# Small attention matmuls of a hybrid decoder step on one core: head pairs, key pages and column groups issued side by side

## The chip, the core and the metric

The kernel runs on one core of a Trainium2 chip. A core has a matrix engine (TensorE, PE in the profile; its weight loads are listed apart, as PEld), VectorE (DVE), ScalarE (ACT), GpSimd (POOL), a queue engine that starts transfers (SP), and 16 DMA engines. Operands lie in SBUF, matmul results in PSUM, which has eight banks of 128 partitions by 512 fp32 columns. The metric is the device time of one execution, in microseconds; lower is better. Before the change it is 897.04 us (median of three runs, 896.72 to 897.54).

## The reference

One decoder layer for 512 prompt tokens and for 8 sequences that each add 4 tokens to 1024 cached ones. Three causal branches work on the same input and are merged by gates; a SwiGLU feed-forward follows. What matters here is the pooling branch's projection and the stick-breaking attention:

```
br_a = einsum('btgc,gcd->btgd', p, pool_w) * pool_scale        # 4 groups, 64 channels each
z    = einsum('bqhd,bkhd->bhqk', q, k) * HEAD_DIM**-0.5 + sb_bias
log_rest = where(mask, log_sigmoid(-z), 0)                     # mask: k_pos < q_pos
log_pass = cumsum(log_rest, axis=3, reverse=True) - log_rest
a    = where(mask, exp(log_sigmoid(z) + log_pass), 0)
o    = einsum('bhqk,bkhd->bqhd', a, v)                         # 8 heads of 64
merged = gate0 * br_a + gate1 * (o @ w_att_o) + gate2 * br_c
```

For the prompt the keys are the prompt's own, in blocks of 128 queries. For the 8 sequences they are 8 pages of 128 keys from a paged cache and the 4 new ones.

## The kernel before

**Large matmuls.** Nearly all of TensorE's work goes through one helper, `gemm` (the matmul of L223). An fp32 product is made of three passes in a rounded fp32 type: weight high part by data high part, high by low, low by high. Weights are streamed: a raw tile is loaded from HBM, ACT makes its high part (L131), DVE its low part (L132), and the two wait in one of three buffers. Data is held for all 544 tokens (32 sample tokens, then 512 of the prompt) and used in two halves of 288 and 256 columns. In the profile these are the rows `mm<-xh,wh`, `mm<-xl,wh`, `mm<-xh,wl`.

**Order.** The code is recorded in program order, and a scheduler then sets the order of each engine's instructions once, at build time, by its own picture of when each is ready. On the chip every engine takes its list from the front; an instruction that waits holds up what is behind it on that engine. Large matmuls that are ready are placed between the small ones of the attention.

**PSUM.** While the branches run, the eight banks are three for `mm`, two for `z`, two for `tp` and one for `o`.

**Projection of the pooling branch** (L492 to L501). Four groups contract over 64 channels only. For each of 8 output chunks and both halves of the tokens three matmuls (L499) of 64 rows go into a `z` bank, and ACT scales the result into `mg` (L501). Groups 0 and 2 lie in rows 0 to 63, groups 1 and 3 in rows 64 to 127. DVE meanwhile makes the depthwise convolution, one tap at a time (L426, `acc`).

**Prompt attention** (L553 to L608). A unit is a pair of heads and a block of 128 queries; 16 units. `front` makes the scores of the two heads `s`, three matmuls each over 64 rows (L564), head 0 in rows 0 to 63 and head 1 in rows 64 to 127, each into a `z` bank; DVE adds bias and mask (L565), then come logs, a reversed running sum (L572) and an exponential. `back`, one unit later, transposes the weights of each head (L583), ACT copies them (L584), and per head and key block a matmul (L586) makes 64 output rows of the one `o` bank. fp32 matmuls show as two rows each in the profile.

**Sample attention** (L619 to L729). For each sequence `k_load` fetches the keys in four tiles `kr`, each with two indirect transfers of 128 x 512 fp32 (256 KB) issued by POOL (L623); there are six such buffers, so one sequence and a half. `v_load` fetches the values in two tiles `vr` of 1 MB (L630), two buffers. `sample_front` makes the scores: for each of four head pairs `hp` and four tiles `jj` a matmul (L654) with 32 output rows, `jj` choosing which 32 (a column group of the array). `sample_back` makes the output from eight key blocks in the same four column groups (L680), and the new tokens' values as one matmul of 32 rows by 512 columns into the fourth group (L681). L668 and L687 are small matmuls of the running sum and of the head selection. Gate matmuls (L223) of the other branches run in between.

Of the kernel before, what the change touches and what calls it, by code (L numbers as in the profile page):

```python
# [146 lines left out]
def hybrid_layer_kernel(  # L147
# [14 lines left out]
           "z": psA.enter_context(pool("z", 2, space=PSUM)),  # L162
# [5 lines left out]
    def bank(tag="mm"):  # L168
        return pst[tag].tile([P, 512], F32, tag=tag, name=tag)

    def auxb():
        return bank("tp")

# [52 lines left out]
    # constants  # L226
# [266 lines left out]
    for mo in range(KD):  # L493
        g, m = mo // 2, mo % 2
        rs = 64 * (g % 2)
        for c0, c1 in HALVES:
            ps = bank("z")
            for n_, (a, b) in enumerate(((pw[0], ph_), (pw[0], pl_), (pw[1], ph_))):
                nc.tensor.matmul(ps[:, :c1 - c0], a[rs:rs + 64, g // 2, m * P:(m + 1) * P], b[rs:rs + 64, g // 2, c0:c1],  # L499
                                 start=n_ == 0, stop=n_ == 2)  # L500
            nc.scalar.mul(mg[:, mo, c0:c1], ps[:, :c1 - c0], vcol(V_PS + mo))  # L501
# [51 lines left out]
    def front(ap, hp, i, q_, k_):  # L553
# [4 lines left out]
        rc = ap.tile([P, 2, wd], F32, tag=f"rc{i % 2}", bufs=1, name=f"rc{hp}{i}", padded_shape=[P, 2, P * (3 + i % 2)])  # L558
        for s in range(2):
            r = slice(64 * s, 64 * s + 64)  # L560
            zp = bank("z")
            qs = slice(i * P, (i + 1) * P)
            for n_, (a, b) in enumerate(((qh, kh), (qh, kl), (ql, kh))):
                nc.tensor.matmul(zp[:, :wd], a[r, qs], b[r, :wd], start=n_ == 0, stop=n_ == 2)  # L564
            nc.vector.scalar_tensor_tensor(out=zt[:, s], in0=zp[:, :wd], scalar=vcol(V_SB + 2 * hp + s),  # L565
                                           in1=cc_(C_ME + NP - wd, wd), op0=ALU.add, op1=ALU.add)
# [10 lines left out]
    def back(ap, hp, i, rc, vtok):  # L577
        op_ = bank("o")
        for s in range(2):
            tp = bank("tp").rearrange("p (k c) -> p k c", k=4)  # L580
            at = ap.tile([P, 4, P], F32, tag="at", bufs=3, name=f"at{hp}{i}{s}")
            for kb in range(i + 1):
                nc.tensor.transpose(tp[:, kb], rc[:, s, kb * P:(kb + 1) * P], ident)  # L583
            nc.scalar.copy(at[:, :i + 1], tp[:, :i + 1])  # L584
            for kb in range(i + 1):
                nc.tensor.matmul(op_[64 * s:64 * s + 64, :P], vtok[:, kb, 64 * s:64 * s + 64], at[:, kb], start=kb == 0, stop=kb == i)  # L586
# [49 lines left out]
    def new_keys():  # L636
        znf = sp.tile([32, 256], F32, name="znf")
        znt = sp.tile([32, 256], F32, name="znt")
        zp = bank("z")
# [10 lines left out]
    def sample_front(b):  # L650
        zp = bank("z")
        for hp in range(4):
            for jj in range(4):
# [22 lines left out]
    def sample_back(b, at):  # L676
        op_ = bank("o")
        for j in range(8):
            c = j % 4
            nc.tensor.matmul(op_[32 * c:32 * c + 32], at[:, j], kvt[b, "v", j // 4][:, j % 4], start=j < 4, stop=j >= 4 and c < 3)  # L680
        nc.tensor.matmul(op_[96:128], at[96:128, 8], vs96[96:128], start=False, stop=True)  # L681
# [394 lines left out]
```

## Time and profile before

| | |
|---|---|
| median of three runs | 897.04 us |
| profiled execution, first to last instruction | 899.0 us |
| PE busy | 877.0 us (98%) |
| DVE, ACT, POOL busy | 478.1, 348.5, 134.8 us |
| share of the chain that ended last on PE | 96% |

The page's own span, 899.0 us, is 2.0 us above the median of the runs; sums below are made against the span and then set against the median. PE counts as busy from a matmul's start to its modelled end, and matmuls overlap, so a busy PE is not one that could take no more: what a matmul costs its successors is read from the distance between starts. The stages, from the timeline: input projections to about 47 us; the pooling projection between large matmuls, 47 to 78 us; prompt attention, 90 to 235 us; sample attention, 240 to 400 us; attention output, output projection and norm, to 501 us; feed-forward, to the end.

### The profile page before, as it was taken

The page shows a single profiled execution, that of the slowest core. Times are in us where ns is not written, and L with a number is a line of the kernel's source. Part 1 is how long each engine was busy: PE and PEld are TensorE (multiplying, and loading weights), DVE is VectorE, ACT ScalarE, POOL GpSimd, SP SyncE. Part 2 cuts the span into 40 slices and gives each one's busy share as a digit, 9 for nine tenths or more (in the row PEclk, how much of TensorE's full clock was granted, in tenths as well). Part 3 has the DMA queues.
Part 4 walks back from the last instruction along what each step waited for, and adds up shares of the span by engine and source line. Part 5 has one row for each costly group of instructions (what it writes and reads, how often), then busy time and mean ns, then how long its engine had stood idle before and what let it go on. Part 6 is the DMA issues. An engine that isn't in the chain of part 4 may idle for free.

```text
span 899.0 us, 16259 instructions
## 1 busy us (share of the span) xinstructions
PE 877.0 (98%) x6889; PEld 811.0 (90%) x6889; DVE 478.1 (53%) x845; ACT 348.5 (39%) x583; POOL 134.8 (15%) x158
## 2 busy tenths in 40 slices
PE   7999999999999999999999999999999999999993
PEld 6999999887886667779999999999999999999993
DVE  4899886887343454449646433333333333334437
ACT  5445377776533315244513333232323232222211
POOL 1430100005257476310001000000000000000002
PEclk9999999999999999999999999999999999999997
DMA  9314323214648688646610122233232322323322
GB/s 291 118 34 115 96 73 113 65 38 137 214 143 289 238 290 291 229 136 225 207 48 1 48 68 76 92 95 94 94 95 94 95 58 73 101 75 83 96 81 100
DMA packets 96393, 110.36 MB, mean 123 GB/s; under 512 B 4416, under 2 KB 88224, under 8 KB 94144
## 3 DMA queue, kind: packets, MB, share of 16 engines
q1 hardware_dynamic: 87840, 73.12, 26.4%
q0 software_dynamic: 8480, 36.20, 11.9%
q8 instruction: 54, 0.88, 0.4%
q14 instruction: 19, 0.16, 0.1%
HBM read 104.44 MB, written 4.87 MB: 122 GB/s over the span
## 4 chain that ended last, share of the span: by engine, by line
PE 96%; DVE 2%; ACT 1%; DMA 1%; issue 0%; SPq 0%; another core or an unknown queue 0%; DVEq 0%; ACTq 0%
PE mm L223 82%; PE z L654 3%; PE o L680 2%; PE z L564 2%; PE o L586 2%; PE tp L583 1%; PE tp L795 1%; PE o L681 1%; PE z L499 1%; DMA raw<-in_w_in 1%; PE tp L861 1%; DVE y L999 0%; DVE y L991 0%; PE tp L687 0%; DVE rc L572 0%
## 5 line engine op out<-in xcount | busy, mean ns | idle before, releaser
L132 DVE TENSOR_TENSOR wl<-raw,wh 128x1024 fp32r<-128x1024 f32 (+1 forms) x129 | 152.3, 1184 | 137.7 <-ACT wh L131 136.5
L131 ACT CAST wh<-raw 128x1024 fp32r<-128x1024 f32 (+1 forms) x129 | 129.3, 1006 | 238.9 <-PE mm L223 212.2
L223 PE MATMUL mm<-xh,wh 128*128 128x256 f32 (+1 forms) x672 | 198.3, 295 | 5.7 <-ACT wh L131 5.6
L223 PE MATMUL mm<-x1l,wh 128*128 128x288 f32 (+1 forms) x704 | 202.7, 288 | 0.0
L223 PE MATMUL mm<-x1h,wl 128*128 128x288 f32 (+1 forms) x704 | 201.4, 287 | 0.0
L223 PE MATMUL mm<-x1h,wh 128*128 128x288 f32 (+1 forms) x704 | 200.5, 286 | 0.1
L223 PE MATMUL mm<-xl,wh 128*128 128x256 f32 (+1 forms) x672 | 198.1, 295 | 0.2 <-DVE xl L210 0.2
L223 PE MATMUL mm<-xh,wl 128*128 128x288 f32 (+1 forms) x672 | 197.0, 294 | 0.7 <-issue 0.7
L223 PEld LDWEIGHTS mm<-xh,wh 128*128 128x128 f32 x672 | 127.9, 191 | 16.9 <-issue 9.8
L223 PEld LDWEIGHTS mm<-xl,wh 128*128 128x128 f32 x672 | 127.8, 190 | 8.6 <-issue 7.3
L223 PEld LDWEIGHTS mm<-xh,wl 128*128 128x128 f32 x672 | 127.5, 190 | 8.6 <-issue 7.7
L223 PEld LDWEIGHTS mm<-x1l,wh 128*128 128x128 f32 x704 | 132.2, 188 | 0.2
L223 PEld LDWEIGHTS mm<-x1h,wh 128*128 128x128 f32 x704 | 132.0, 188 | 0.4 <-ACT sg L905 0.3
L223 PEld LDWEIGHTS mm<-x1h,wl 128*128 128x128 f32 x704 | 132.0, 188 | 0.0
L223 PE MATMUL mm<-gl,wh 128*128 128x256 f32 (+1 forms) x352 | 101.7, 289 | 0.0
L223 PE MATMUL mm<-gh,wh 128*128 128x256 f32 (+1 forms) x352 | 101.3, 288 | 0.0
L223 PE MATMUL mm<-gh,wl 128*128 128x256 f32 (+1 forms) x352 | 100.8, 286 | 0.0
L623 POOL DMA_INDIRECT kr<-in_ck,pix x64 | 67.6, 1056 | 44.7 <-PE z L654 20.6
L908 DVE TENSOR_TENSOR sg<-mm,sg 128x288 f32<-128x288 f32 (+1 forms) x44 | 19.4, 441 | 91.8 <-PE mm L223 91.8
L223 PEld LDWEIGHTS mm<-gl,wh 128*128 128x128 f32 x352 | 66.1, 188 | 0.1
L223 PEld LDWEIGHTS mm<-gh,wh 128*128 128x128 f32 x352 | 66.2, 188 | 0.0
L223 PEld LDWEIGHTS mm<-gh,wl 128*128 128x128 f32 x352 | 66.1, 188 | 0.0
(216 smaller groups left out, 1202.8 us busy)
## 6 DMA issues: line engine op xcount, KB each, us to landing
raw<-in_w_in SPq DMA_DIRECT2D x14, 1024.0 KB, 8.2
raw<-in_w_g SPq DMA_DIRECT2D x11, 1024.0 KB, 5.3
raw<-in_w_u SPq DMA_DIRECT2D x11, 1024.0 KB, 5.4
raw<-in_w_d SPq DMA_DIRECT2D x16, 512.0 KB, 4.0
raw<-in_w_in SPq DMA_DIRECT2D x12, 512.0 KB, 3.9
raw<-in_w_out SPq DMA_DIRECT2D x4, 1024.0 KB
raw<-in_w_d SPq DMA_DIRECT2D x8, 384.0 KB, 4.3
raw<-in_w_att_o SPq DMA_DIRECT2D x4, 512.0 KB, 3.4
```

Source lines behind the costliest of these rows:

```text
L131: self.nc.scalar.copy(hi[:, a:b], v[:, a:b])
L132: self.nc.vector.tensor_tensor(out=lo[:, a:b], in0=v[:, a:b], in1=hi[:, a:b].bitcast(F32), op=ALU.subtract)
L223: ins = nc.tensor.matmul(ps[:, :n], lw, rr, start=first and s == 0, stop=last and s == len(steps) - 1)
L499: nc.tensor.matmul(ps[:, :c1 - c0], a[rs:rs + 64, g // 2, m * P:(m + 1) * P], b[rs:rs + 64, g // 2, c0:c1], start=n_ == 0, stop=n_ == 2)
L564: nc.tensor.matmul(zp[:, :wd], a[r, qs], b[r, :wd], start=n_ == 0, stop=n_ == 2)
L583: nc.tensor.transpose(tp[:, kb], rc[:, s, kb * P:(kb + 1) * P], ident)
L586: nc.tensor.matmul(op_[64 * s:64 * s + 64, :P], vtok[:, kb, 64 * s:64 * s + 64], at[:, kb], start=kb == 0, stop=kb == i)
L623: nc.gpsimd.indirect_dma_start(out=kr[:, u].rearrange("p h c -> p (h c)"), out_offset=None, in_=ck, in_offset=bass.IndirectOffsetOnAxis(ap ...
L654: nc.tensor.matmul(zp[32 * jj:32 * jj + 32, :256], qbd[:, hp, b], kvt[b, "k", jj][:, :, hp], start=hp == 0, stop=hp == 3)
L680: nc.tensor.matmul(op_[32 * c:32 * c + 32], at[:, j], kvt[b, "v", j // 4][:, j % 4], start=j < 4, stop=j >= 4 and c < 3)
L681: nc.tensor.matmul(op_[96:128], at[96:128, 8], vs96[96:128], start=False, stop=True)
L908: nc.vector.tensor_tensor(out=sg, in0=pu[:, :n], in1=sg, op=ALU.mult)
```

## The change

Five edits. The pool `z` has one buffer, a tile of two banks (`pair`), in place of two of one bank; `new_keys` and `sample_front` use its first bank. The pooling projection takes the two groups of a pair of row halves together: for each of three passes first the one group, then the other, and the second group's result is scaled by DVE, not ACT. `front` issues pass by pass over both heads, not head by head. `back` makes both heads' transposes and copies first (four `at` buffers, not three) and then the output matmuls block by block over both heads, head 1 first. `sample_front` takes the tiles `jj` in the order 3, 2, 1, 0, `sample_back` the second value tile before the first, and the new tokens' values are four matmuls of 128 columns, one per column group. The deleted comment lines of the diff are left out here.

```diff
-           "z": psA.enter_context(pool("z", 2, space=PSUM)),
+           "z": psA.enter_context(pool("z", 1, space=PSUM)),
...
+    def pair():
+        return pst["z"].tile([P, 2, 512], F32, tag="z", name="z")
...
-    for mo in range(KD):
-        g, m = mo // 2, mo % 2
-        rs = 64 * (g % 2)
-        for c0, c1 in HALVES:
-            ps = bank("z")
-            for n_, (a, b) in enumerate(((pw[0], ph_), (pw[0], pl_), (pw[1], ph_))):
-                nc.tensor.matmul(ps[:, :c1 - c0], a[rs:rs + 64, g // 2, m * P:(m + 1) * P], b[rs:rs + 64, g // 2, c0:c1],
-                                 start=n_ == 0, stop=n_ == 2)
-            nc.scalar.mul(mg[:, mo, c0:c1], ps[:, :c1 - c0], vcol(V_PS + mo))
+    for gp in range(2):
+        for m in range(2):
+            for hf, (c0, c1) in enumerate(HALVES):
+                zz = pair()
+                pss = [zz[:, s] for s in range(2)]
+                for n_, (a, b) in enumerate(((pw[0], ph_), (pw[0], pl_), (pw[1], ph_))):
+                    for s in range(2):
+                        r = slice(64 * s, 64 * s + 64)
+                        nc.tensor.matmul(pss[s][:, :c1 - c0], a[r, gp, m * P:(m + 1) * P], b[r, gp, c0:c1], start=n_ == 0, stop=n_ == 2)
+                for s in range(2):
+                    mo = 4 * gp + 2 * s + m
+                    if s:
+                        nc.vector.tensor_scalar(mg[:, mo, c0:c1], pss[s][:, :c1 - c0], vcol(V_PS + mo), None, op0=ALU.mult)
+                    else:
+                        nc.scalar.mul(mg[:, mo, c0:c1], pss[s][:, :c1 - c0], vcol(V_PS + mo))
...
+        zz = pair()
+        zps = [zz[:, s] for s in range(2)]
+        qs = slice(i * P, (i + 1) * P)
+        for n_, (a, b) in enumerate(((qh, kh), (qh, kl), (ql, kh))):
+            for s in range(2):
+                r = slice(64 * s, 64 * s + 64)
+                nc.tensor.matmul(zps[s][:, :wd], a[r, qs], b[r, :wd], start=n_ == 0, stop=n_ == 2)
...
+        for kb in range(i + 1):
+            for s in (1, 0):
+                nc.tensor.matmul(op_[64 * s:64 * s + 64, :P], vtok[:, kb, 64 * s:64 * s + 64], ats[s][:, kb], start=kb == 0, stop=kb == i)
...
-            for jj in range(4):
+            for jj in (3, 2, 1, 0):
...
-        for j in range(8):
+        for j in (4, 5, 6, 7, 0, 1, 2, 3):
             c = j % 4
-            nc.tensor.matmul(op_[32 * c:32 * c + 32], at[:, j], kvt[b, "v", j // 4][:, j % 4], start=j < 4, stop=j >= 4 and c < 3)
-        nc.tensor.matmul(op_[96:128], at[96:128, 8], vs96[96:128], start=False, stop=True)
+            nc.tensor.matmul(op_[32 * c:32 * c + 32], at[:, j], kvt[b, "v", j // 4][:, j % 4], start=j >= 4, stop=False)
+        for c in range(4):
+            f = slice(P * c, P * c + P)
+            nc.tensor.matmul(op_[32 * c:32 * c + 32, f], at[96:128, 8], vs96[96:128, f], start=False, stop=True)
```

What the scheduler makes of it is shown at three places. In the changed kernel `gemm`'s matmul is L226, and the others are named as they come.

TensorE, sample attention, the scores of the fourth sequence (`kr_3080`, `3083`, `3086`, `3089` are its four key tiles in order; L680 and L681 belong to the second sequence's output). Before:

```order
L654 MATMUL z<-kr_3080,qbd 32x256
...
L654 MATMUL z<-kr_3083,qbd 32x256
...
L680 MATMUL o<-vr_2807,sat_2762 32x512 x4
...
L680 MATMUL o<-vr_2809,sat_2762 32x512 x4
L681 MATMUL o<-vs_95,sat_2762 32x512
...
L654 MATMUL z<-kr_3086,qbd 32x256
...
L654 MATMUL z<-kr_3089,qbd 32x256
L654 MATMUL z<-kr_3080,qbd 32x256
```

And in the changed kernel, the same sequence's scores (tiles `kr_3059` to `kr_3068`) and the second sequence's output:

```order
L694 MATMUL o<-vr_2788,sat_2738 32x512 x4
L694 MATMUL o<-vr_2786,sat_2738 32x512 x4
L697 MATMUL o<-vs_95,sat_2738 32x128 x4
...
L668 MATMUL z<-kr_3068,qbd 32x256
L668 MATMUL z<-kr_3065,qbd 32x256
L668 MATMUL z<-kr_3062,qbd 32x256
L668 MATMUL z<-kr_3059,qbd 32x256
L668 MATMUL z<-kr_3068,qbd 32x256
```

Before, the first matmul on each key tile stood alone between large matmuls wherever its tile was expected, and 13 followed together; now all 16 follow each other behind the last tile, and so do the eight output matmuls with the new values.

TensorE at the end of the pooling projection (L504 is its matmul, `L574` that of the prompt scores, the rest large matmuls), in the changed kernel:

```order
L226 MATMUL mm<-xl,wh_852 128x288
L226 MATMUL mm<-xh,wl_853 128x288
L504 MATMUL z<-ph,wh_457 128x288 x2
L504 MATMUL z<-pl,wh_457 128x288 x2
L504 MATMUL z<-ph,wl_458 128x288 x2
L504 MATMUL z<-ph,wh_457 128x256 x2
L504 MATMUL z<-pl,wh_457 128x256 x2
L504 MATMUL z<-ph,wl_458 128x256 x2
L574 MATMUL z<-kh_981,qh_917 128x128 x2
L226 MATMUL mm<-xh,wh_852 128x256
```

Before, each chunk's two halves of three stood together in this way (first half, then second, in two `z` buffers) with 22 to 28 large matmuls to the next chunk. Now a set is six, between most sets stand 21 to 55 large matmuls, and the last two sets and the first scores stand next to each other, all three in the one two-bank tile.

VectorE over the same place, in the changed kernel (L508 is the new scaling of the second group, `acc` the convolution's taps, `wl` the low part of a weight, `ql` of a query):

```order
L508 TENSOR_SCALAR mg<-z,vt 128x288
L429 SCALAR_TENSOR_TENSOR acc_111<-ge_109,vt,acc_111 128x512
L429 SCALAR_TENSOR_TENSOR acc_112<-ge_110,vt,acc_112 128x512
...
L132 TENSOR_TENSOR wl_985<-raw_923,wh_984 128x1024
L429 SCALAR_TENSOR_TENSOR acc_111<-ge_109,vt,acc_111 128x512
L508 TENSOR_SCALAR mg<-z,vt 128x256
L216 SCALAR_TENSOR_TENSOR ql_918<-mm,qh_917 128x256
```

The two scalings are those of the last two sets: between them now stand five taps and one weight split. Before, none of these scalings was on VectorE.

## Rows read from the trace of the kernel before

**Rows 1.** The page: its span and part 1, busy time of each engine.

```profile
span 899.0 us, 16259 instructions
...
PE 877.0 (98%) x6889; PEld 811.0 (90%) x6889; DVE 478.1 (53%) x845; ACT 348.5 (39%) x583; POOL 134.8 (15%) x158
```

**Rows 2.** Chain in time order: start us, duration, engine, tile, line.

```profile
47.02 0.93 PE z L499 x6
...
501.00 265.40 PE mm L223 x2136
```

**Rows 3.** Windows: stretch, PE PEld DVE ACT POOL busy (x), PEclk, DMA share, GB/s.

```profile
47.00:90.00 43.00, 43.00 (x322) 40.92 (x322) 40.65 (x56) 22.11 (x40) 5.82 (x6) 1.00 0.27 78
90.00:237.00 147.00, 146.48 (x1132) 130.36 (x1132) 113.09 (x207) 102.14 (x195) 24.52 (x31) 1.00 0.34 109
237.00:401.00 164.00, 162.45 (x1278) 118.92 (x1277) 74.74 (x136) 54.98 (x65) 79.37 (x80) 1.00 0.66 222
```

**Rows 4.** Timeline of VectorE, 52 to 85 us: start, duration, line, operation.

```profile
52.23 1.17 DVE L416 TENSOR_REDUCE acc<-prs 128x32 f32<-128x992 f32 x1
...
81.11 1.22 DVE L132 TENSOR_TENSOR wl<-raw,wh 128x1024 fp32r<-128x1024 f32 x1
82.24 0.75 DVE L426 SCALAR_TENSOR_TENSOR acc<-ge,vt,acc 128x512 f32<-128x512 f32 x1
82.91 1.35 DVE L489 TENSOR_TENSOR mg<-mg,gt 128x544 f32<-128x544 f32 x2
```

**Rows 5.** Groups by form, VectorE: count, busy us, mean ns, idle before, releasers.

```profile
L482 DVE TENSOR_SCALAR gt<-mm,vt 128x288 f32<-128x288 f32 x18 | 9.3, 514 | 18.6 <-PE mm L223 7.5 <-PE o L680 6.1 <-PE z L654 2.9
```

**Rows 6.** Windows, the last 10 us of the execution; columns as in rows 3.

```profile
889.00:899.00 10.00, 0.00 (x0) 0.00 (x0) 6.46 (x9) 0.00 (x0) 0.92 (x1) 0.50 0.41 153
```

**Rows 7.** Chain in time order, prompt scores and prompt output.

```profile
126.96 0.90 PE z L564 x6
...
184.96 0.89 PE z L564 x3
...
187.32 1.02 PE o L586 x8
```

**Rows 8.** Timeline of TensorE, one set of prompt scores.

```profile
126.89 0.51 PE L564 MATMUL z<-kh,qh 64*128 64x512 f32 x2
127.23 0.40 PE L564 MATMUL z<-kl,qh 64*128 64x512 f32 x2
```

**Rows 9.** Timeline of TensorE, prompt output of a block whose two heads alternate.

```profile
223.41 0.66 PE L586 MATMUL o<-at,vtok 128*64 128x128 f32 x8
```

**Rows 10.** Timeline of TensorE, sample scores: a lone visit, then a whole set.

```profile
288.80 0.29 PE L223 MATMUL mm<-xl,wh 128*128 128x288 f32 x1
289.02 0.62 PE L654 MATMUL z<-kr,qbd 128*32 128x256 f32 x2
289.57 0.40 PE L223 MATMUL mm<-xh,wl 128*128 128x288 f32 x1
289.81 0.29 PE L223 MATMUL mm<-xh,wh 128*128 128x288 f32 x1
...
305.11 1.92 PE L654 MATMUL z<-kr,qbd 128*32 128x256 f32 x28
306.96 0.39 PE L223 MATMUL mm<-xh,wh 128*128 128x256 f32 x1
```

**Rows 11.** Chain in time order, sample output, its new values, and the head selection.

```profile
365.16 0.99 PE o L680 x8
...
370.13 0.97 PE o L681 x2
...
387.33 0.36 PE tp L687 x8
```

**Rows 12.** Windows, 20 us with key and value loads; columns as in rows 3.

```profile
280.00:300.00 20.00, 18.58 (x128) 12.27 (x121) 7.23 (x14) 6.66 (x8) 12.56 (x15) 1.00 0.95 343
```

**Rows 13.** Timeline of GpSimd, one key load; in brackets its idle time before.

```profile
308.15 1.01 POOL L623 DMA_INDIRECT kr<-in_ck,pix  x1 [0.30 <-issue]
```

More of the change, by code (lines that the diff above doesn't have):

```diff
@@ L558, in front @@
         rc = ap.tile([P, 2, wd], F32, tag=f"rc{i % 2}", bufs=1, name=f"rc{hp}{i}", padded_shape=[P, 2, P * (3 + i % 2)])
-        for s in range(2):
[L560 to L565, printed above, removed]
+        zz = pair()
[5 more added lines that the diff above has]
+                nc.tensor.matmul(zps[s][:, :wd], a[r, qs], b[r, :wd], start=n_ == 0, stop=n_ == 2)
+        for s in range(2):
+            nc.vector.scalar_tensor_tensor(out=zt[:, s], in0=zps[s][:, :wd], scalar=vcol(V_SB + 2 * hp + s),
                                            in1=cc_(C_ME + NP - wd, wd), op0=ALU.add, op1=ALU.add)
@@ L578, in back @@
         op_ = bank("o")
+        ats = []
         for s in range(2):
             tp = bank("tp").rearrange("p (k c) -> p k c", k=4)
-            at = ap.tile([P, 4, P], F32, tag="at", bufs=3, name=f"at{hp}{i}{s}")
+            at = ap.tile([P, 4, P], F32, tag="at", bufs=4, name=f"at{hp}{i}{s}")
             for kb in range(i + 1):
@@ L584, in back @@
             nc.scalar.copy(at[:, :i + 1], tp[:, :i + 1])
-            for kb in range(i + 1):
-                nc.tensor.matmul(op_[64 * s:64 * s + 64, :P], vtok[:, kb, 64 * s:64 * s + 64], at[:, kb], start=kb == 0, stop=kb == i)
+            ats.append(at)
+        for kb in range(i + 1):
+            for s in (1, 0):
+                nc.tensor.matmul(op_[64 * s:64 * s + 64, :P], vtok[:, kb, 64 * s:64 * s + 64], ats[s][:, kb], start=kb == 0, stop=kb == i)
         o0 = NS + i * P
@@ L638, in new_keys @@
         znt = sp.tile([32, 256], F32, name="znt")
-        zp = bank("z")
+        zp = pair()[:, 0]
         for hp in range(4):
@@ L650, in sample_front @@
     def sample_front(b):
-        zp = bank("z")
+        zp = pair()[:, 0]
         for hp in range(4):
-            for jj in range(4):
+            for jj in (3, 2, 1, 0):
                 nc.tensor.matmul(zp[32 * jj:32 * jj + 32, :256], qbd[:, hp, b], kvt[b, "k", jj][:, :, hp],
```

## The prediction

> **What bounds the kernel now.** I read part 1 of the page first: TensorE is busy for 877.0 of 899.0 us [rows 1]. The reader should then look at the chain of waits, which is TensorE for 96% (the table above). Its long last piece, 265.40 us for 2136 large matmuls [rows 2], gives 0.124 us for one with nothing between. The windows come third: in each of the three stages that the change touches TensorE is busy almost throughout [rows 3]. So the time falls by what leaves TensorE's list, and rises by any wait put in it. Counting the large matmuls of a stage and taking 0.124 us for each leaves about 9 us of small work in the pooling projection, 54 in prompt attention and 64 in sample attention. The change can act on these. All terms are made against the span, 899.0 us; the profiled execution is 2.0 us above the median of the runs, and I subtract that at the end.
>
> Going from large matmuls to a small one and back costs something beyond the small one. A lone visit of the sample scores shows it [rows 10]: from the start of the large matmul ahead (288.80) to that of the second one behind (289.81) are 1.01 us; two large ones are 0.26 of that (at 288 columns they follow each other at 0.13), so the visit costs 0.75, for one score matmul (two rows). A whole set of 14, 28 rows, costs 1.85 from its start to the next large matmul, and with 0.2 of entry 2.05 [rows 10]. The price is in the visit, not in the matmul.
>
> **The change part by part.**
>
> A. *Pooling projection.* Before, eight chunks each show 0.93 us for six matmuls [rows 2], all one behind another. With 0.2 for the visit that is 8 x 1.13 = 9.0. After, eight sets of six, in which the matmuls on rows 0 to 63 and on 64 to 127 alternate. What two row halves together cost is in rows 8: a pair of 512 columns follows the next at 0.34 and 0.23 us, so a pair of 272 at about 0.15 to 0.18. Three pairs and the visit are 0.75, eight are 6.0. Term: -3.0 (bounds -2 and -4.5).
>
> B. *The second group's scaling on VectorE.* VectorE is busy for 40.65 of these 43.00 us, ScalarE for 22.11 [rows 3]. The scalings stand in VectorE's list among the convolution's taps, and with the tile's one buffer each set of the projection, and the first prompt scores behind the eighth, wait for the scaling before. The first scaling stands just ahead of the sum that started at 52.23 [rows 4]; I put its end at 52.7. From there to the end of the eighth the new list has 39 taps at 0.67 (start to start, 82.24 to 82.91 [rows 4]), 26.1; six weight splits at 1.13 [rows 4], 6.8; four gate products at 0.64 [rows 4], 2.5; seven scalings. For a scaling there is no row; a same-shaped pass from PSUM with a column of constants takes 514 ns [rows 5], less the 0.08 by which such passes overlap (0.75 against 0.67 for a tap), 0.44, so 3.1. The sum of L416 and two small ones are 1.7. Total 40.2, end at 92.9. TensorE could be at those scores at 47.0 + 264 large matmuls of the new list x 0.124 (32.7) + eight sets (6.0) = 85.7. Term: +7.2, a wait of TensorE for VectorE, mainly ahead of the last set and of the first scores (which stand next to each other). Bounds: 0, if the list's large matmuls also run later, so that taps are done in the slack, and +10, if weight splits behind the taps come late as well.
>
> The Trainium skill, in "TensorEngine Tiling (Array Packing)", section "PSUM Bottleneck", says that packing speeds up TensorE but not the copy out of PSUM, and that both ScalarE and VectorE should do that copy. The first half is what term B says; against the second stands that here VectorE has 2.35 us left of 43 and ScalarE 20.9 [rows 3]. By the advice the sum would be without B; by the rows it is with it.
>
> C. *Clock.* The granted clock is 1.00 in all three stretches [rows 3], and 0.50, the 1.2 GHz level, where TensorE had no matmul for 10 us [rows 6]. No row shows a pause of a few us. If the pause of B drops it, a large matmul costs another 0.124 us. Bounds 0 and +3 (24 large matmuls at the lower level); I take +0.8.
>
> D. *Prompt attention.* Scores: three matmuls of one head, standing alone, take 0.89 us, and six of both heads 0.90 [rows 7]: two row halves together are free of charge. But ten of the sixteen units already have the six together, and there the engine pairs the heads by itself: the two first-pass matmuls of both heads come first [rows 8], though the order has head 0's three before head 1's. So only six units gain, 0.7 each at their mean width (384 columns): -4.2. Output: eight rows of one head after the other took 1.02 [rows 7], eight that alternate 0.66 [rows 9], 0.045 for each row. Of 160 rows some 90 do not alternate now: -4.0. New waits: a unit's output now needs both heads' copies by ScalarE, and its scores both halves of the one tile, whose reuses have only 13 to 24 large matmuls (1.6 to 3.0 us) between them, while VectorE is busy for 113.09 of 147.00 [rows 3]. Bounds 0 and +6, taken +2, since most reuses have more than the two passes of VectorE need. Term: -6.2 (-9 to -2).
>
> E. *Key pages.* Before, the timeline has 18 lone visits like the one of rows 10 beside the sets, at 0.75. After, the scores of a sequence stand together, in two cases in two pieces, and the matmuls that made the lone visits add little to a set: -13.5 (-15 to -11).
>
> F. *Values.* Before, a sequence's output is two halves of four key blocks, 0.99 each [rows 11], and the new values 0.97 [rows 11] because they use one column group. With 0.2 for each of two visits, 3.35. After, one visit of 8 + 4. The four new-value matmuls on four column groups have as nearest row eight small rows at 0.36 [rows 11]: 0.3. So 0.2 + 1.9 + 0.3 = 2.4, and -0.95 x 8 = -7.6 (-9 to -5).
>
> G. *Loads of keys and values.* The starts of whole score sets lie some 18 us apart in the timeline; E and F take 2.6 us from each sequence (21.1 / 8), to some 15. Before, the stretch moved 222 GB/s [rows 3], and 343 in the 20 us where key and value loads were under way, with the DMA engines at 0.95 [rows 12]. A sequence needs 4.2 MB of keys and values and about 1 MB of weights, 5.2 MB, at 343 GB/s 15.2 us. Also the last key buffers come free only when the whole set is done, not page by page, so the next sequence's third and fourth tiles are issued later. POOL issues a load in 1.01 + 0.30 [rows 13], ten of them 13 us, and has 79.37 us of work in this stage [rows 3]; it does not bind alone. Term: +3.5 (0 to +11).
>
> Sum: -3.0 + 7.2 + 0.8 - 6.2 - 13.5 - 7.6 + 3.5 = -18.8. Span 880.2, median 878.
>
> **The rivals.**
>
> R1, no wait for VectorE. The scalings would be done in VectorE's slack, or the projection's sets would come later by themselves. Then B and C are nothing: 878 - 8 = 870. For it: the bound of B at zero. Against: 40.65 of 43.00 busy [rows 3], and the list adds work in front of the split weights.
>
> R2, the heads were not paired before. The Trainium skill, "TensorE: Matmul & The Clock Gate", Part 3 under "What overlaps and what doesn't", says that matmuls start and end strictly in the order of the program. Rows 8 disagree: both heads' first-pass matmuls start ahead of head 0's second. Were the order kept, all sixteen units would gain: 48 pairs at a mean 320 columns save 0.133 each (half of the pair's 0.27 without sharing, scaled from 0.34 to 0.23 at 512), 6.4, and six visits 1.2, together 7.6 in place of 4.2: 874.6.
>
> R3, sample attention is bound by its page loads. Each sequence then takes 15.2 us plus what the late third and fourth tile lose; G goes to +11, and the time is 885.5. For it: 0.95 of the DMA engines busy [rows 12]. Against: the mean of the stage is 0.66 [rows 3], and six key buffers hold one sequence and a half.
>
> R4, slower: the single score tile. If in prompt attention each of the 16 units' scores waits for VectorE to have read the unit before, with VectorE's weight splits of 1.13 us ahead of it in the list, the waits add up; they decide from (18.8 + 2.0) / 16 = 1.3 us for each unit, beyond the 0.1 that D has, and at 1.5 us the time is 901. For it: VectorE at 113.09 of 147.00 [rows 3] and one tile in place of two banks. Against: 1.6 to 3.0 us of large matmuls between most reuses.
>
> **How the numbers follow.** Forecast 55%, 878 us; by the bounds of its terms, which do not all go one way, 871 to 886. R1 15%, R3 20%, R2 5%, R4 5%. The range that should hold the time 8 times in 10 takes R1 and R3 in with their neighbourhood: 866 to 890. Less than 0.2% is about what a measurement of this kernel cannot tell from no change; only R4 and mishaps of its size reach it: faster 93%, same 2%, slower 5%.
>
> **What would show it right or wrong.** In the profile after: windows of 47 to 95 us with VectorE without idle time and TensorE with several us of it, ended by the scaling of `mg` or by `ql` (B; without it R1); PEclk below 1.00 just behind (C). Prompt scores as pairs in every unit and `o` rows alternating at 0.055 (D); TensorE's waits at `z` for the bias pass of over 1 us per unit would be R4. Sample scores only in sets near 2 us, outputs at 2.4 (E, F). TensorE waiting for `kr` or `vr` at the sets, with DMA near 0.95, would be G, and over 8 us of it R3. I am wrong above 890 or below 866, and wrong in the working if stages other than these three change by more than 1 us.

## The result, and the profile after

The changed kernel takes 883.21 us (median of four runs, 882.96 to 884.88) against 896.89 for the kernel before: 0.9846 of it, 95% interval 0.9832 to 0.986. It is faster by 13.7 us, inside the range, and 5 us short of the forecast.

The page of the changed kernel, its span and part 1; rows 1 answer to it:

```profile
span 881.2 us, 16355 instructions
...
PE 847.7 (96%) x6937; PEld 801.6 (91%) x6937; DVE 476.0 (54%) x853; ACT 344.7 (39%) x575; POOL 135.4 (15%) x158
```

Its three stages, in windows of the changed kernel (columns as in [rows 3]):

```profile
45.80:95.00 49.20, 42.41 (x329) 39.76 (x328) 49.16 (x73) 19.35 (x33) 6.15 (x7) 0.92 0.23 68
95.00:235.00 140.00, 139.27 (x1131) 125.86 (x1132) 104.89 (x193) 100.95 (x192) 23.89 (x30) 0.99 0.34 109
235.00:385.00 150.00, 144.52 (x1342) 118.52 (x1337) 73.24 (x144) 59.08 (x69) 81.77 (x82) 0.99 0.72 250
```

Where [rows 3] had TensorE busy almost throughout, the first stretch now leaves it 6.8 us idle beside a VectorE that is busy for 49.16 of 49.20, and the third leaves it 5.5 us idle. The waits of TensorE in the changed kernel say for what. These are the longest behind the kernel's start (what waited, what it waited for: total us, times, longest):

```profile
PE z L574 <- DVE mg L508: 4.3, 1, 4.3
PE o L694 <- DMA vr<-in_cv,piv: 3.2, 2, 3.0
PE z L504 <- DVE mg L508: 1.7, 2, 1.2
PE z L668 <- DMA kr<-in_ck,pix: 1.2, 1, 1.2
```

The first and the third are the wait of term B, the other two, 4.4 us, those of term G. TensorE's timeline at the end of the pooling projection shows B, and what it does to the clock:

```profile
84.70 0.40 PE L504 MATMUL z<-ph,wh 64*128 64x288 f32 x2
...
86.61 0.39 PE L504 MATMUL z<-ph,wh 64*128 64x256 f32 x2 [1.24 <-DVE mg L508]
...
91.54 0.48 PE L574 MATMUL z<-kh,qh 64*128 64x128 f32 x2 [4.31 <-DVE mg L508]
...
95.15 0.41 PE L226 MATMUL mm<-xl,wh 128*128 128x256 f32 x1
95.36 0.41 PE L226 MATMUL mm<-xh,wl 128*128 128x256 f32 x1
```

VectorE over the same place:

```profile
86.05 0.51 DVE L508 TENSOR_SCALAR mg<-z,vt 128x288 f32<-128x288 f32 x1
86.47 2.73 DVE L429 SCALAR_TENSOR_TENSOR acc<-ge,vt,acc 128x512 f32<-128x512 f32 x4
89.12 1.22 DVE L132 TENSOR_TENSOR wl<-raw,wh 128x1024 fp32r<-128x1024 f32 x1
90.26 0.74 DVE L429 SCALAR_TENSOR_TENSOR acc<-ge,vt,acc 128x512 f32<-128x512 f32 x1
90.92 0.48 DVE L508 TENSOR_SCALAR mg<-z,vt 128x256 f32<-128x256 f32 x1
```

The last set ended on TensorE at about 87.2; between its last two scalings VectorE had five taps and a weight split, and TensorE stood until 91.5. Behind that pause large matmuls of 256 columns start 0.213 us apart (95.15 to 95.36) instead of 0.117. From 92 to 97 us the granted clock is 0.50, the lower of its two levels; 24 of these matmuls fall under it, which costs 2.3 us.

The small work itself, in the chain of the changed kernel in order of time:

```profile
169.63 0.89 PE z L574 x6
...
192.09 1.02 PE o L600 x16
...
251.14 1.99 PE z L668 x32
...
277.84 9.72 DMA vr<-in_cv,piv
...
339.83 1.85 PE o L694 x16
```

Sixteen rows of prompt output take the 1.02 us that eight took [rows 7]; a sequence's scores are one visit of 32 rows in 1.99; its eight value blocks take 1.85, 0.99 twice before [rows 11]. The new values, in TensorE's timeline:

```profile
319.80 1.92 PE L694 MATMUL o<-vr,sat 128*32 128x512 f32 x16 [0.22 <-DMA vr<-in_cv,piv]
321.66 0.42 PE L697 MATMUL o<-vs,sat 32*32 32x128 f32 x8
```

0.42 us in place of 0.97 [rows 11].

To see what each stage gave, I take for every trace the time from one landmark to the next (first projection matmul of the pooling branch, first prompt score, first sample score, last head selection) and subtract its large matmuls at their undisturbed pace, 0.117 us for 256 columns and 0.130 for 288. What is left is small work, waits and lost clock, in us (s_old, p_act and the others are the experiments below):

| trace | pooling projection | prompt | sample | TensorE idle in sample |
|---|---|---|---|---|
| before | 9.4 | 55.0 | 65.7 | 1.6 |
| changed | 13.0 | 50.8 | 49.4 | 4.5 |
| s_old | 13.0 | 50.6 | 63.2 | 0.0 |
| p_act | 6.6 | 47.5 | 48.0 | 4.6 |
| z_two | 10.2 | 51.5 | 50.9 | 5.8 |
| before_again | 9.4 | 55.3 | 67.0 | 2.9 |
| after_again | 13.0 | 51.7 | 62.2 | 9.3 |
| p_act_again | 6.6 | 49.7 | 59.6 | 8.2 |
| pa_noload | 6.9 | 52.3 | 42.4 | 0.0 |

The lost clock behind the pause of B falls into the prompt column. The idle time of 1.6 us in the first row is nearly all of a kind that the traces of the changed kernel and of the first set do not have: stops that the profile puts down to "issue", in which TensorE waits for nothing that it shows:

```profile
PE mm L223 <- issue: 0.7, 1, 0.7
PE z L654 <- issue: 0.6, 2, 0.3
```

They come up again in the second and third set.

### The profile page after: what moved, and what is told of

It reads as the page before. It is cut to its first block, busy times and chain, and to the rows that moved or that the text cites. A ratio compares the mean times of both kernels' runs of the same rounds, so it can differ in the third digit from the quotient of the medians.

```text
span 881.2 us, 16355 instructions
## 1 busy us (share of the span) xinstructions
PE 847.7 (96%) x6937; PEld 801.6 (91%) x6937; DVE 476.0 (54%) x853; ACT 344.7 (39%) x575; POOL 135.4 (15%) x158
## 3 DMA queue, kind: packets, MB, share of 16 engines
q0 software_dynamic: 8480, 36.20, 11.6%
## 4 chain that ended last, share of the span: by engine, by line
PE 87%; DVE 7%; DMA 2%; issue 2%; POOL 1%; ACT 1%; SPq 0%; DVEq 0%; ACTq 0%; POOLq 0%
PE mm L226 77%; DVE acc L429 3%; PE z L668 2%; PE o L694 1%; PE z L574 1%; PE o L600 1%; PE tp L595 1%; DVE wl L132 1%; DMA vr<-in_cv,piv 1%; POOL kr L637 1%; PE tp L811 1%; DMA kr<-in_ck,pix 1%; DMA raw<-in_w_in 1%; PE tp L877 1%; DVE y L1015 0%
## 5 line engine op out<-in xcount | busy, mean ns | idle before, releaser
L226 PE MATMUL mm<-xh,wh 128*128 128x256 f32 (+1 forms) x672 | 199.2, 297 | 7.6 <-ACT wh L131 5.8
L226 PE MATMUL mm<-x1l,wh 128*128 128x288 f32 (+1 forms) x704 | 202.7, 288 | 0.0
L226 PE MATMUL mm<-x1h,wl 128*128 128x288 f32 (+1 forms) x704 | 201.4, 287 | 0.0
L226 PE MATMUL mm<-x1h,wh 128*128 128x288 f32 (+1 forms) x704 | 200.5, 286 | 0.1
L226 PE MATMUL mm<-xl,wh 128*128 128x256 f32 (+1 forms) x672 | 197.4, 294 | 0.2 <-DVE xl L213 0.2
L226 PE MATMUL mm<-xh,wl 128*128 128x288 f32 (+1 forms) x672 | 197.5, 295 | 0.0
L226 PEld LDWEIGHTS mm<-xh,wh 128*128 128x128 f32 x672 | 129.0, 192 | 13.0 <-ACT wh L131 6.2
L226 PEld LDWEIGHTS mm<-x1l,wh 128*128 128x128 f32 x704 | 132.2, 188 | 0.2
L226 PEld LDWEIGHTS mm<-xl,wh 128*128 128x128 f32 x672 | 128.7, 192 | 3.9 <-issue 2.9
L226 PEld LDWEIGHTS mm<-x1h,wh 128*128 128x128 f32 x704 | 132.0, 188 | 0.4 <-ACT sg L921 0.3
L226 PEld LDWEIGHTS mm<-x1h,wl 128*128 128x128 f32 x704 | 132.0, 188 | 0.0
L226 PEld LDWEIGHTS mm<-xh,wl 128*128 128x128 f32 x672 | 128.6, 192 | 3.3 <-issue 2.6
L226 PE MATMUL mm<-gl,wh 128*128 128x256 f32 (+1 forms) x352 | 101.7, 289 | 0.0
L226 PE MATMUL mm<-gh,wh 128*128 128x256 f32 (+1 forms) x352 | 101.3, 288 | 0.0
L226 PE MATMUL mm<-gh,wl 128*128 128x256 f32 (+1 forms) x352 | 100.8, 286 | 0.0
L637 POOL DMA_INDIRECT kr<-in_ck,pix x64 | 69.5, 1086 | 35.8 <-issue 14.9
L226 PEld LDWEIGHTS mm<-gl,wh 128*128 128x128 f32 x352 | 66.1, 188 | 0.1
L226 PEld LDWEIGHTS mm<-gh,wh 128*128 128x128 f32 x352 | 66.2, 188 | 0.0
L226 PEld LDWEIGHTS mm<-gh,wl 128*128 128x128 f32 x352 | 66.1, 188 | 0.0
```

The costliest lines, as they stand in the source:

```text
L226: ins = nc.tensor.matmul(ps[:, :n], lw, rr, start=first and s == 0, stop=last and s == len(steps) - 1)
L637: nc.gpsimd.indirect_dma_start(out=kr[:, u].rearrange("p h c -> p (h c)"), out_offset=None, in_=ck, in_offset=bass.IndirectOffsetOnAxis(ap ...
```

## The experiments

They ran in three sets, each on one chip. The kernel before took 897.25 us beside the first set, 902.69 beside the second and 902.93 beside the third. So kernels are compared within a set, or by their ratio to the kernel before.

**p_act** (first set): ScalarE scales both groups.

```diff
                 for s in range(2):
                     mo = 4 * gp + 2 * s + m
-                    if s:
-                        nc.vector.tensor_scalar(mg[:, mo, c0:c1], pss[s][:, :c1 - c0], vcol(V_PS + mo), None, op0=ALU.mult)
-                    else:
-                        nc.scalar.mul(mg[:, mo, c0:c1], pss[s][:, :c1 - c0], vcol(V_PS + mo))
+                    nc.scalar.mul(mg[:, mo, c0:c1], pss[s][:, :c1 - c0], vcol(V_PS + mo))
```

> Changed kernel with one edit: ScalarE, not VectorE, also scales the second group of the pooling projection. Theory (VectorE's taps ahead of the scaling hold the two-bank tile): in the changed kernel's trace the waits of the projection's sets and of the first prompt scores for VectorE (1.2 + 1.2 + 4.3 us), the wait for the last query weight behind them and 24 large matmuls at the 1.2 GHz level (0.213 instead of 0.117 us, 2.4) add to 9.6 us; they go, and the time is 883.2 - 9.6 = 873.6 (871.5 to 876). Rival (the set's two scalings now follow each other on ScalarE behind weight casts of 1.0 us, and TensorE waits there at each of 8 sets for 0.5 to 1 us): 879 to 882.

Measured: 874.71 us (873.15 to 879.64), 0.9761 of the kernel before (0.9737 to 0.9785). The windows of p_act over the pooling projection:

```profile
47.00:90.00 43.00, 43.00 (x345) 40.75 (x345) 42.57 (x59) 23.37 (x41) 5.89 (x6) 1.00 0.26 78
```

TensorE is busy throughout at the full clock, though VectorE is still busy for 42.57 of 43.00: it is no longer between two sets. The edit is worth 8.5 us against the first measurement of the changed kernel (7.6 by the two ratios); 9.6 were expected. B and C together are shown. The eight sets are now spread, 27 to 30 large matmuls apart, and their stage costs 6.6 us instead of 9.4.

**z_two** (first set): two score tiles of one bank, as before, VectorE's scaling kept.

```diff
-           "z": psA.enter_context(pool("z", 1, space=PSUM)),
+           "z": psA.enter_context(pool("z", 2, space=PSUM)),
...
-                zz = pair()
-                pss = [zz[:, s] for s in range(2)]
+                pss = [bank("z") for s in range(2)]
...
-        zz = pair()
-        zps = [zz[:, s] for s in range(2)]
+        zps = [bank("z") for s in range(2)]
...
-        zp = pair()[:, 0]
+        zp = bank("z")
...
```

> Changed kernel with the scores' PSUM pool as before: two tiles of one bank each in place of one tile of two banks; orders and VectorE's scaling stay. Theory (the loss needs both: VectorE's late scaling and one tile that only comes free as a whole): with separate banks the sets of the projection are split and spread, the eighth scaling stands behind 32 taps instead of 45, waits of 2 to 4 us remain and the clock does not fall: 877 (874 to 880). Rival 1 (VectorE alone, whatever the tile): 882 to 884. Rival 2 (the tile alone): 873 to 874.

Measured: 883.24 us (882.78 to 884.0), 0.9842 (0.9829 to 0.9856), the same as the changed kernel. The number is that of the first rival, but its reason isn't there: TensorE has no wait for the scaling in this trace. The sets are split into two of three matmuls where VectorE is late; the stage costs 10.2 instead of 13.0, and no clock is lost behind it. So the theory's 877 missed, though its loss is gone. The table shows where that went: the changed kernel differs by the tile alone, and against it prompt attention costs 3.0 more, once the 2.3 us of lost clock are taken off its column, and sample attention 1.5. So the two-bank tile earns some 4.5 us in the attention and loses about as much to VectorE's late reading in the projection.

**s_old** (first set): the three edits of sample attention undone.

```diff
-            for jj in (3, 2, 1, 0):
+            for jj in range(4):
...
-        for j in (4, 5, 6, 7, 0, 1, 2, 3):
+        for j in range(8):
             c = j % 4
-            nc.tensor.matmul(op_[32 * c:32 * c + 32], at[:, j], kvt[b, "v", j // 4][:, j % 4], start=j >= 4, stop=False)
-        for c in range(4):
-            f = slice(P * c, P * c + P)
-            nc.tensor.matmul(op_[32 * c:32 * c + 32, f], at[96:128, 8], vs96[96:128, f], start=False, stop=True)
+            nc.tensor.matmul(op_[32 * c:32 * c + 32], at[:, j], kvt[b, "v", j // 4][:, j % 4], start=j < 4, stop=j >= 4 and c < 3)
+        nc.tensor.matmul(op_[96:128], at[96:128, 8], vs96[96:128], start=False, stop=True)
```

> Changed kernel with the three edits of sample attention undone (key tiles in the order 0 to 3, value blocks 0 to 7, new values as one matmul in one column group). Theory (visits to TensorE's small work are what is saved, and most of it is not lost to loads): the sample stage gives back the 15 us that lie between the two traces there: 898 (895 to 901). Rival (the stage is bound by its page loads either way): 884 to 888.

Measured: 895.99 us (895.63 to 899.0), 0.999 (0.998 to 1.0). These edits are worth 12.8 us, nearly the whole gain of the change; what pooling projection and prompt attention lose and win cancels to about 1 us. The sample stage goes from 49.4 to 63.2, and TensorE has no idle time in it, which the windows of s_old show:

```profile
237.00:397.00 160.00, 160.00 (x1266) 117.29 (x1265) 72.46 (x138) 57.46 (x66) 78.64 (x80) 1.00 0.67 227
```

So the waits for kr and vr are made by the shorter stage: term G.

**att_old** (first set): prompt scores and output head by head again, inside the two-bank tile.

```diff
...
-        for n_, (a, b) in enumerate(((qh, kh), (qh, kl), (ql, kh))):
-            for s in range(2):
-                r = slice(64 * s, 64 * s + 64)
-                nc.tensor.matmul(zps[s][:, :wd], a[r, qs], b[r, :wd], start=n_ == 0, stop=n_ == 2)
         for s in range(2):
...
+            zp = zz[:, s]
...
+            for n_, (a, b) in enumerate(((qh, kh), (qh, kl), (ql, kh))):
+                nc.tensor.matmul(zp[:, :wd], a[r, qs], b[r, :wd], start=n_ == 0, stop=n_ == 2)
...
-            at = ap.tile([P, 4, P], F32, tag="at", bufs=4, name=f"at{hp}{i}{s}")
+            at = ap.tile([P, 4, P], F32, tag="at", bufs=3, name=f"at{hp}{i}{s}")
...
-        for kb in range(i + 1):
-            for s in (1, 0):
-                nc.tensor.matmul(op_[64 * s:64 * s + 64, :P], vtok[:, kb, 64 * s:64 * s + 64], ats[s][:, kb], start=kb == 0, stop=kb == i)
+            for kb in range(i + 1):
+                nc.tensor.matmul(op_[64 * s:64 * s + 64, :P], vtok[:, kb, 64 * s:64 * s + 64], at[:, kb], start=kb == 0, stop=kb == i)
```

> Changed kernel with the order of prompt scores and prompt output undone (head by head), the two-bank tile and four weight buffers kept. Theory (six of sixteen units' scores and about 90 of 160 output rows did not share the array before): 883.2 + 6 to 7.5 = 890 (888 to 892). Rival (the engine overlaps the heads by itself, the order gives nothing): 883 to 885.

Measured: 909.34 us (908.72 to 910.5), 1.0139 (1.0123 to 1.0154): 26 us above the changed kernel, far from both expectations. Windows of att_old at the end of prompt attention:

```profile
225.00:260.00 35.00, 30.32 (x182) 22.64 (x181) 21.21 (x35) 22.97 (x41) 13.08 (x15) 0.86 0.34 103
```

In the new order of TensorE's list the scores fall behind the large matmuls, and after the last of these 18 score matmuls, 28 transposes and 28 output matmuls of the last units stand in one piece with no large matmul between; TensorE waits there for ScalarE and VectorE, at a mean clock of 0.86. The edit changed the schedule more than the sharing of the array, so it doesn't measure D. It shows that the head-by-head order doesn't go with the tile of two banks. The expectation of att_old says that four weight buffers were kept; the run has three `at` buffers, as the kernel before. att_z2_old below has three as well, and no such piece.

**p_act_z2** and **att_z2_old** (second set): p_act with two tiles of one bank, and the same with the prompt's order of the kernel before.

```diff
-           "z": psA.enter_context(pool("z", 1, space=PSUM)),
+           "z": psA.enter_context(pool("z", 2, space=PSUM)),
...
-        zz = pair()
-        zps = [zz[:, s] for s in range(2)]
+        zps = [bank("z") for s in range(2)]
...
```

The second also has

```diff
-        zps = [bank("z") for s in range(2)]
-        qs = slice(i * P, (i + 1) * P)
-        for n_, (a, b) in enumerate(((qh, kh), (qh, kl), (ql, kh))):
-            for s in range(2):
-                r = slice(64 * s, 64 * s + 64)
-                nc.tensor.matmul(zps[s][:, :wd], a[r, qs], b[r, :wd], start=n_ == 0, stop=n_ == 2)
         for s in range(2):
+            r = slice(64 * s, 64 * s + 64)
+            zp = bank("z")
+            qs = slice(i * P, (i + 1) * P)
+            for n_, (a, b) in enumerate(((qh, kh), (qh, kl), (ql, kh))):
+                nc.tensor.matmul(zp[:, :wd], a[r, qs], b[r, :wd], start=n_ == 0, stop=n_ == 2)
...
```

and the output order and the three `at` buffers of att_old's diff.

> As p_act (ScalarE scales both groups), with two score tiles of one bank each in place of one of two banks. Theory (z_two lost in prompt and sample attention, 2.8 and 1.4 us by the traces, what it gained in the pooling projection; without VectorE's scaling only the loss is left): 874.7 + 3 to 4 = 878 (876.5 to 880). Rival (the tile matters only through VectorE's late scaling): 874.7 within 1.

> As p_act_z2, with prompt scores and prompt output in the order of the kernel before (head by head, each head its own bank); four weight buffers kept. att_old put the head-by-head order into the one two-bank tile and so made a head wait for the other's bank; here that is avoided. Theory (term D): 6 to 7.5 us above p_act_z2, about 885. Rival (the engine overlaps the heads by itself): within 1.5 us of p_act_z2.

Measured: p_act_z2 894.61 us (891.23 to 897.88), 0.9904 (0.9881 to 0.9926); att_z2_old 897.0 (890.88 to 901.38), 0.9935 (0.9909 to 0.996). The difference, 2.4 us, has the sign of D and is within the intervals: inconclusive. The runs of these two spread by 7 to 10 us. The expected 878 was worked out for the first chip; by the ratios p_act_z2 is some 6 us slower than p_act_again of the third set, more than the 3 to 4 expected, but that compares two chips. TensorE's waits in the trace of p_act_z2 name what the first set did not have:

```profile
PE mm L226 <- issue: 9.9, 17, 1.7
...
PE z L663 <- issue: 1.9, 3, 0.8
```

These are stretches in which TensorE waited for nothing that the profile shows.

**p_act_k7** (second set): seven key buffers.

```diff
-KRB = 6
+KRB = 7
```

> As p_act, with seven key buffers in place of six. Theory (GpSimd's queue paces the loads: ten issues a sequence at 1.27 us, the value loads behind eight key loads that wait for buffers): with a seventh buffer the waits for kr and vr (4.5 us in the trace of p_act) shrink and output and next scores stand together, one visit less for five sequences: 870 (867 to 872). Rival (the bytes of the pages bind the stage): 874 to 876.

Measured: 891.98 us (891.69 to 892.21), 0.9882 (0.9863 to 0.99). Without p_act beside it on that chip the expected step can't be read from the total; against p_act_again's 0.9838 on a chip that reads alike it is no gain. Its trace has no wait for kr or vr, but 7.7 us put down to issue in this stage, and a pause of 6.6 us for VectorE. Whether a seventh buffer would help on the chip of the first set stays open.

**before_again** (second set): the kernel before, unchanged.

> The kernel before, unchanged, for a second profile. Its first profile spans 899.0 us, above the median of 897.0, while the changed kernel's profiled run spans 1.8 us less than its time. Theory (the first profile was of an execution some 3 to 4 us longer than the usual one): span 895, time 897. Rival (the kernel before always spans about 2 us more than its time): span 899.

Measured: 901.78 us, ratio 0.9997 (0.998 to 1.0013). Its profiled run took 901.54 us and spans

```profile
span 899.8 us, 16259 instructions
```

1.8 us less than its time, as the changed kernel's does (881.2 of 882.96). The rival is refuted: the first profile of the kernel before, 899.0 us, was then of an execution of about 900.8 us, 3.9 above its median. The theory's 895 and 897 were not met, as this chip takes 902 us for the kernel. And a second reading is left: 900.8 us is above all 15 runs of this kernel beside the first set (895.66 to 899.23) and among those beside the second (900.5 to 905.95), and that profile has the stops put down to issue. So it can be a usual execution on a chip of the slower kind; the record doesn't say where it was taken.

**after_again**, **p_act_again**, **pa_keys_old**, **pa_noload** (third set). The last two are p_act with the key tiles in the old order, and p_act with the first sequence's pages for all eight (the other key and value loads are left out, with GpSimd's issuing of them, and four key buffers do in place of six):

```diff
-            for jj in (3, 2, 1, 0):
+            for jj in range(4):
```

```diff
-KRB = 6
+KRB = 4
...
     def k_load(b):
+        if b:
+            for jj in range(4):
+                kvt[b, "k", jj] = kvt[0, "k", jj]
+            return
...
     def v_load(b):
+        if b:
+            for u in range(2):
+                kvt[b, "v", u] = kvt[0, "v", u]
+            return
```

> The changed kernel itself, so that the other three have it on the same chip. By the first measurement 0.985 of the kernel before. On the chip of the second set, where the kernel before took 902.7 us, TensorE had waits put down to issue during the page loads; if this chip is such a one, a smaller gain (0.988 to 0.995), if not, 0.985 again.

> p_act once more, beside the changed kernel on one chip. Theory (VectorE's late scaling costs the same 9 us on any chip): 8 to 10 us below after_again. Rival (the difference was one of runs): within 3 us of after_again.

> p_act with the key tiles taken in the order 0 to 3 again; the order of values and the four new-value matmuls stay. Theory (term E: lone visits come back, 13.5 us, and the waits for kr and vr, 4.6 us with about 1 us of lower clock behind them, go): 8 us above p_act (6 to 11). Rival (most of the gain of sample attention is in the values): 0 to 3 us above p_act.

> p_act with the pages of the first sequence used for all eight: the key and value loads of the other seven are left out, all matmuls stay. Theory (term G: what is left of waits in sample attention is for page loads): its waits for kr and vr, 4.6 us, and about 1 us of lower clock go, and output and scores that stand together save another 1 us: 6 to 7 us below p_act; no waits put down to issue in this stage. Rival (the waits come from the order of TensorE's list, not from the loads): within 2 us of p_act.

Measured, beside 902.93 us for the kernel before:

| kernel | median us | ratio to before | 95% interval |
|---|---|---|---|
| after_again | 897.78 | 0.995 | 0.9929 to 0.997 |
| p_act_again | 888.44 | 0.9838 | 0.9812 to 0.9865 |
| pa_keys_old | 891.75 | 0.987 | 0.9848 to 0.9893 |
| pa_noload | 872.85 | 0.9651 | 0.963 to 0.9672 |

The changed kernel gains 5 us here, not 14, the least of what was expected on such a chip. p_act is 9.3 us below it, much as in the first set, and the trace of after_again has the same waits for VectorE's scaling, 4.3 and 1.7 us: B and C do not depend on the chip. The sample stage is what differs: 62.2 us in the table against 49.4 for the same program. Windows of after_again, and then of the changed kernel's first profile, over 20 us of page loads:

```profile
320.00:340.00 20.00, 15.72 (x125) 11.13 (x123) 6.83 (x15) 6.66 (x8) 9.40 (x12) 0.83 0.85 300
```

```profile
320.00:340.00 20.00, 18.78 (x176) 16.03 (x172) 8.56 (x18) 8.00 (x10) 14.15 (x15) 1.00 1.04 384
```

300 GB/s here against 384 there, and a lower clock. What TensorE does in such a stretch, in the timeline of p_act_again:

```profile
270.29 1.55 PE L665 MATMUL z<-kr,qbd 128*32 128x256 f32 x14
272.63 0.65 PE L665 MATMUL z<-kr,qbd 128*32 128x256 f32 x4 [0.79 <-issue]
274.07 0.64 PE L665 MATMUL z<-kr,qbd 128*32 128x256 f32 x4 [0.79 <-issue]
275.54 1.02 PE L665 MATMUL z<-kr,qbd 128*32 128x256 f32 x10 [0.83 <-issue]
276.49 0.41 PE L226 MATMUL mm<-xh,wh 128*128 128x288 f32 x1
```

One set of scores stops three times for 0.8 us with its data there, and takes 6.2 us to the next large matmul, where a set took 1.99 in the first trace. Only 2.4 of this is idle time, so the idle time in the table, 8.2 here against 4.6 on the first chip, understates what the stops cost: the stage is 11.6 us longer. Without the loads all of this is gone from the stage, as the windows of pa_noload show:

```profile
240.00:300.00 60.00, 60.00 (x615) 45.72 (x617) 32.09 (x64) 22.62 (x30) 2.67 (x8) 1.00 0.18 58
```

pa_noload is 15.6 us below p_act_again, where 6 to 7 were expected from the first chip's waits, and its sample stage, 42.4, is 5.6 below that of p_act on the first chip (48.0), which is the size expected. Against p_act_again the stage falls by 17.2, and the prompt column rises by 2.6 for waits on ScalarE. Its TensorE list is also another one than p_act's, with 83 large matmuls fewer in the stage, so not all of the difference need be the loads. pa_keys_old is only 3.3 us above p_act_again, the intervals overlap, and 8 were expected: here what the order of the key tiles saves seems mostly taken back by the stops, 8.2 us idle against 3.6. Why TensorE stops was not measured; shown is that in this stage the stops need the page loads (the transfers or their issuing on GpSimd, which were left out together). One stop, of 0.76 us, is left in pa_noload, at 216 us, before the stage and while the first sequence's pages come in. The stops are strong on the chips of the second and third set, absent from the five traces of the changed kernel and the first set, and weak, 1.3 us, in the first trace of the kernel before. Whether the chip itself makes the difference, or what else ran on it, is not on record.

## Why the prediction was right, and where it missed

**A** (-3.0): right. p_act, where nothing waits, has 6.6 in the stage, 9.4 before: -2.8.

**B** (+7.2): right in place, cause and size. TensorE's idle time from the projection's first set to the first scores is 6.6 us, 5.5 of it at the two places named, and p_act takes it away. R1 was worked out as this kernel without B and C, 870; built as p_act, that is 874.7, the other errors included.

**C** (+0.8, bounds 0 and +3): mis-sized. 24 large matmuls at 0.213 instead of 0.117 us are 2.3, near the upper bound. The row used for it, the last 10 us of the execution, had said only that the clock can fall.

**D** (-6.2): right in size, but half of it came from where none was expected. The prompt column falls by 4.2 to the changed kernel, in which 2.3 are C, so that D is -6.5, and by 7.5 to p_act. By itself, on the total, it was not measured: att_old changed the schedule, and att_z2_old is within the spread. But the kept traces show it. For each visit to small work between the first prompt score and the first sample score I take the time from the start of the large matmul ahead to that of the second one behind, less two large ones and less idle time. With the old order these add up to 53.1 us, in before, before_again and att_z2_old alike; in the changed kernel to 45.6 and in p_act to 45.0; with the new order on tiles of one bank to 49.9 (z_two) and 49.0 (p_act_z2). att_old has 66.2, 22 of them in its one long piece. So order and tile together save 7.5 to 8.1, about the 8.2 that D gave to its two gains, and roughly half of it comes only with the two-bank tile, which D counted as a cost. The waits that D put at +2, and that R4 needs, did not come: no prompt score waits for VectorE's bias pass in the list of waits, and 13 to 108 large matmuls stand between one unit's scores and the next one's, not 13 to 24. For R2 there is [rows 8] alone, and no run here decides it further.

**E and F** (-21.1) **with G** (+3.5): s_old to changed is 63.2 to 49.4, -13.8, against -17.6. G was mis-sized. In the changed kernel's trace the waits for pages cost 6.4 us, of which 4.4 are idle time: 4.6 at the first late value tile, with the lower clock behind it (granted 0.50 from 289 to 292 us), 1.5 at the late key tile, 0.3 at a second value tile. That leaves -20.2 for E and F. F was nearly exact: an output visit without a wait costs 2.40, as worked out, and the new values 0.42; one of the eight costs 1.1 more, without a wait, because other small work stands in the middle of it. On the third set's chip more is lost than even R3 had: the stage of the same program is 12.8 us longer there, and the gain is 5 us, where R3's 885.5 would be 11.5. But TensorE is stopped there by nothing that the profile names, rather than by kr or vr. The forecast had G as a supply of bytes; in the trace of the changed kernel GpSimd's list comes first: the late value tile's 9.72 us of load began behind eight key loads in a row. That is one wait's history; no run on that chip tests it.

**Span and median.** The prediction took 2.0 us off the span to come to the median. before_again and the changed kernel show the reverse, the span lies 1.8 below the time, so the profile of before was of a long execution or of a slower chip. The sum set against that profile's own span misses by only 1.0 (880.2, measured 881.2), but that is luck: the profile that it starts from is of an execution 3.9 us longer than the kernel's median, and the changed kernel's is of a usual one. Set against the median the sum gives 897.0 - 18.8 = 878.2, the same forecast, and a miss of 5.0 us. By the table 3.8 of it are in sample attention (G 2.9, E and F 0.9) and 1.2 in the prompt column (C 1.5, D 0.3 the other way), the projection is 0.6 better, and 0.6 no step accounts for. Outside the three stages the two traces differ by -1.1 ahead of them and +0.4 behind. The prediction had called more than 1 us a sign of an error, but the first 40 large matmuls, which the change leaves alone, vary by 1.4 us from trace to trace.

p_act beats both kernels in both sets in which it ran: 0.9761 and 0.9838 of the kernel before, against 0.9846 (first measurement) and 0.995 for the changed kernel.

## What to carry to other kernels

When small matmuls are paired and their PSUM tile grows to hold the pair, the reader of the tile decides the gain: look at what stands ahead of the reading in that engine's list, and give it to the engine that has room. A visit to small work costs more than the work in it, so collecting visits pays, until the transfers behind them set the pace; count those before. A profiled execution can be a long one of its kernel, so compare its span with its own time before a sum is set against it. And a gain can differ from chip to chip, here 14 and 5 us for the same change: measure both kernels side by side on more than one.

## What the runs showed of the hardware

The same program had, on two of the chips, stops of 0.2 to 1.1 us on TensorE, some in the middle of sets whose data was there, put down to issue; two stretches with several of them moved 276 and 300 GB/s. The traces of the changed kernel and of p_act in the first runs, at up to 384 GB/s, have none of these. With the page loads of seven of the eight sequences left out, none was left in sample attention on such a chip either. A pause of 4.3 us on TensorE was followed by 24 large matmuls at the lower clock level. Three score matmuls on rows 0 to 63 and the three behind them in the list on rows 64 to 127 started as pairs [rows 8], and six took no longer than three alone (0.90 and 0.89 us) [rows 7].
